# Hybrid DeltaNet step on one core: preparation steps of consecutive chunks on seven common places per chunk, scan steps behind four of them

## The chip, the core and the metric

The kernel runs as one program on one core of a Trainium2 chip. The metric is the device time in microseconds (us) of one execution; a lower time is better. The engines are named as the profile names them: PE (matmuls; PEld is its weight load), DVE and ACT (elementwise work), POOL, and SP, which issues every DMA of this kernel.

## The reference: what is computed

One layer of a diffusion backbone over 128 context tokens and 2048 latent tokens, 17 tiles of 128 tokens. Half of the mixer is a gated DeltaNet with 4 heads, run over the tokens in both directions; the other half is a gated spatial MLP. A projection, a second norm and a wide squared-ReLU MLP follow. The part that matters here is the DeltaNet:

```python
    a_mat = jnp.where(strict, jnp.einsum('bnhcd,bnhsd->bnhcs', k_beta, k) * decay, 0.0)
    rhs = jnp.concatenate([v * beta, k_beta * jnp.exp(g)[..., None]], axis=-1)
    sol = lax.linalg.triangular_solve(a_mat + jnp.eye(DN_CHUNK, dtype=f32), rhs,
                                      left_side=True, lower=True, unit_diagonal=True)
    u, w = sol[..., :DV], sol[..., DV:]
    qk = jnp.einsum('bnhcd,bnhsd->bnhcs', q, k) * decay
    ...
    def step(S, xs):
        qd, kd, u_c, w_c, qk_c, gl = xs
        v_new = u_c - jnp.einsum('bhck,bhkv->bhcv', w_c, S)
        o = jnp.einsum('bhck,bhkv->bhcv', qd, S) + jnp.einsum('bhcs,bhsv->bhcv', qk_c, v_new)
        S = S * jnp.exp(gl)[..., None, None] + jnp.einsum('bhck,bhcv->bhkv', kd, v_new)
        return S, o
```

For each chunk a triangular matrix is inverted, which does not need the state of the chunk before; then the state is carried on, which does.

## The kernel before

The program has three stages: modulation, norms and the q, k, v projections (to about 440 us); the DeltaNet stage (to about 1265 us); the MLP (to the end). The change lies in the second.

The kernel takes chunks of 128 tokens. A **unit** is one chunk in one direction; `units` holds 34: 17 forward (0 to 16), then 17 backward (17 to 33, the first of them the context tile). Each unit has 17 **preparation steps** (list `prep`, which invert the matrix) and 4 **scan steps** (list `scan`, which carry the state).

- Preparation: two steps that build the matrix (lines 985 to 1010); a transpose (line 1016); five doubling levels for widths 2, 4, 8, 16, 32, each of two steps; and four closing steps (lines 1066 to 1098). The first step of a level, called **Pa1 to Pa5** here, is four matmuls at line 1036, and DVE makes the tile `P` from them at line 1040. The second, **XY1 to XY5**, is eight matmuls at lines 1048 and 1050 that read `P`; ACT then casts `Y` and `X` (lines 1051, 1052), which the next Pa reads. At the end stand **R** (lines 1084, 1085) and **T** (lines 1094, 1095).
- Scan: **s0** (kT by the state; DVE updates `vt` at line 1108), **s1** (T by vt; ACT copies `vn`), **s2** (kt by vn; DVE makes the new state at line 1128), **s3** (16 matmuls at lines 1139 and 1140 that read `qT` and `QK`; this is the output).

Each unit loads its operands by DMA. `kt`, `kT`, `vt` and `qT` have two buffers each, so the `qT` of unit u+2 can be fetched only when s3 of unit u has read its own, and the `kt` of unit u+2 only after s2 of unit u. As soon as `qT` is there DVE multiplies it with the decay (line 1130), and ACT scales `kt` (line 1103).

All other work of the stage is **fill**: the gate and gMLP projections of all tiles, the output projection and the second norm, whose PE part is mostly matmuls of 512 columns at lines 220 to 222 (one group of three for each slice of 128 inputs).

What sets the order: every step is put on a list with a time in units of a chunk (`at(time, fn, kind)`); unit i has its chunk at time i. Before the change the 17 preparation steps of unit i are spread evenly over a window around i (`WINDOWS`: 2.43 chunks long up to unit 17, 2.69 from unit 18 on), and the 4 scan steps over a window of their own (1.57 and 1.18 chunks). The list is sorted by time and issued; a first matmul of fill is ordered behind the preparation or scan step issued last (from time 18 on: behind the fourth last). The recording layer then orders each engine's queue by its own estimate of when things are ready. Each engine works its queue strictly in that order, so an instruction that waits holds all behind it.

```python
            for j, st in enumerate(u["prep"]):
                at(i - w[0] + (j + 0.5) * (w[0] - w[1]) / n, st, "prep")
            spread(i + w[2], i + w[3], [scan_step(i, f) for f in u["scan"]], "chain")
```

Of the kernel before, what the change touches and what calls it, by code (L numbers as in the profile page):

```python
# [21 lines left out]
NT = 17  # L22
# [8 lines left out]
def interleave(*lists):  # L31
# [5 lines left out]
    for _, _, _, s in sorted(order, key=lambda e: e[:3]):  # L37
# [18 lines left out]
AHEAD = 3  # L56
WINDOWS = [2.46, 0.03, -0.51, 1.06, -1.61, 18.16, 17.58, 18.3,
           2.63, -0.06, -0.18, 1.0, 1.36, 1.64, 1.66, 2.66, 3.17, 3.71]


@with_exitstack
def hybrid_step(
# [144 lines left out]
    def w512(name, dt=F32):  # L207
        return wp.tile([P, 512], dt, tag="w", name=name)
# [61 lines left out]
    with ExitStack() as ph:  # L270
# [479 lines left out]
        for bi in range(len(BLOCKS)):  # L750
# [6 lines left out]
            at = {e: n for n, e in enumerate(order)}  # L757
            tile_of = {}
            for n, (gi, h) in enumerate(order):
                u = us[n] if bi == 0 and n < 3 else feature_tile(blk, bi, gi, h)  # L760
# [158 lines left out]
    with ExitStack() as ph:  # L919
# [337 lines left out]
        def o_loads(u):  # L1257
            t = u["t"]
            u["of"], u["ga"] = w512("of"), w512("ga")
            load(out=u["of"], in_=of_d[t * P : (t + 1) * P, :])  # L1260
            load(out=u["ga"], in_=gate_d[t * P : (t + 1) * P, :])
# [74 lines left out]
        def at(time, fn, kind=None):  # L1336
            events.append((time, len(events), fn, kind))

        def spread(t0, t1, steps, kind):
            for j, st in enumerate(steps):  # L1340
                at(t0 + (t1 - t0) * (j + 0.5) / len(steps), st, kind)

        def scan_step(i, f):
            def g():
                u = units[i]
                if "s" not in u:
                    u["s"] = None if i in (0, NT) else units[i - 1]["sn"] if i not in (1, NT + 1) else u["s0"]
                f()
            return g

        def after(i):

            d = 0 if i == 0 else 1
            store(out=new_state[0, 0, d].rearrange("h k v -> k h v"), in_=units[i]["sn"])
            s0 = q32("S", 2)
            load(out=s0, in_=state_delta[0, 0, d].rearrange("h k v -> k h v"))
            units[i + 1]["s0"] = s0

        p2, p3 = WINDOWS[:8], WINDOWS[8:]
        for i, u in enumerate(units):  # L1360
            w = p2 if i <= NT else p3
            at(i - 3 if i > PL else -10, u["prep_loads"])
            at(i - 1, u["scan_loads"])
            n = len(u["prep"])
            for j, st in enumerate(u["prep"]):
                at(i - w[0] + (j + 0.5) * (w[0] - w[1]) / n, st, "prep")
            spread(i + w[2], i + w[3], [scan_step(i, f) for f in u["scan"]], "chain")
            if i in (0, NT):
                at(i + w[2] + (w[3] - w[2]) * 0.7, lambda i=i: after(i))
            if i >= NT:  # L1370
                at(i, lambda u=u: o_loads(u))
                first, second = o_steps(u)
                spread(i + p3[4], i + p3[5], first, "fill")
                spread(i + p3[6], i + p3[7], second, "fill")
                if u["t"] > 8:
                    st = h2_steps(u["t"], pj, fraw, w512, fpart, fhalf, lambda u=u: u["x2"])
                    spread(i + p3[8], i + p3[9] + 0.2, st[:5], "fill")
                    spread(i + p3[9] + 0.2, i + p3[9] + 2.1, st[5:], None)
# [427 lines left out]
    for j, t in enumerate(range(8, -1, -1)):  # L1806
        st = h2_steps(t, bank, lambda: w512("junk"), w512)
# [5 lines left out]
    for p, (o, n, b) in enumerate(seq):  # L1813
        u = units[n]
# [118 lines left out]
```

## Time and profile before

| | |
|---|---|
| median of 3 runs | 2678.39 us (2676.0 to 2682.14) |
| profiled execution | 2678.03 us |
| its span, first to last instruction | 2676.3 us |
| PE busy in the span | 2622.4 us, 98% |
| DVE busy | 1792.8 us, 67% |
| ACT busy | 1245.4 us, 47% |
| granted PE clock, mean | 0.995 |

Idle time of PE is time in which no matmul runs; the views of waits name what it waited for. An idle stretch of DVE or ACT costs nothing by itself, unless a matmul stands behind what they are late with.

### The profile page before, as it was taken

The page shows a single profiled execution, that of the slowest core. Times are in us where ns is not written, and L with a number is a line of the kernel's source. Part 1 is how long each engine was busy: PE and PEld are TensorE (multiplying, and loading weights), DVE is VectorE, ACT ScalarE, POOL GpSimd, SP SyncE. Part 2 cuts the span into 40 slices and gives each one's busy share as a digit, 9 for nine tenths or more (in the row PEclk, how much of TensorE's full clock was granted, in tenths as well). Part 3 has the DMA queues.
Part 4 walks back from the last instruction along what each step waited for, and adds up shares of the span by engine and source line. Part 5 has one row for each costly group of instructions (what it writes and reads, how often), then busy time and mean ns, then how long its engine had stood idle before and what let it go on. Part 6 is the DMA issues. An engine that isn't in the chain of part 4 may idle for free.

```text
span 2676.3 us, 45017 instructions
## 1 busy us (share of the span) xinstructions
PE 2622.4 (98%) x15698; PEld 2187.8 (82%) x15698; DVE 1792.8 (67%) x3694; ACT 1245.4 (47%) x3092; POOL 224.8 (8%) x448
## 2 busy tenths in 40 slices
PE   8999999999999999999999999999999999999998
PEld 5999998788887777788888888888888787888887
DVE  5867656766666778875688885566565556774874
ACT  4655555555554657763355543333242432332441
POOL 3111112111111111110000000000000000000000
PEclk9999999999999999999999999999999999999999
DMA  8867539655454657985868887443369978776772
GB/s 298 278 207 222 187 109 284 193 165 158 155 163 147 209 181 253 288 283 181 291 201 240 247 300 223 114 122 104 106 190 372 326 268 307 268 251 210 235 259 88
DMA packets 569385, 580.89 MB, mean 217 GB/s; under 512 B 35692, under 2 KB 401692, under 8 KB 565574
## 3 DMA queue, kind: packets, MB, share of 16 engines
q1 hardware_dynamic: 569158, 578.03, 67.6%
q8 instruction: 123, 2.02, 0.3%
q14 instruction: 104, 0.85, 0.1%
HBM read 398.14 MB, written 179.74 MB: 216 GB/s over the span
## 4 chain that ended last, share of the span: by engine, by line
PE 86%; DMA 6%; DVE 5%; ACT 1%; issue 1%; SPq 1%; POOL 0%; DVEq 0%; POOLq 0%; ACTq 0%
PE f L222 17%; PE f L220 17%; PE f L221 17%; PE pj L220 6%; PE pj L222 6%; PE pj L221 6%; PE pd L966 3%; PE pm L220 1%; PE pm L221 1%; PE pm L222 1%; PE pt L578 1%; PE pd L1140 1%; PE pd L1139 1%; DMA hop_d<-opL 1%; DMA qT<-qT_d 1%
## 5 line engine op out<-in xcount | busy, mean ns | idle before, releaser
L220 PE MATMUL f<-hop,zH 128*128 128x512 f32 x960 | 376.5, 393 | 1.2 <-ACT zH L1449 1.2
L221 PE MATMUL f<-hop,zH 128*128 128x512 f32 x960 | 377.1, 393 | 0.0
L222 PE MATMUL f<-hop,zL 128*128 128x512 f32 x960 | 376.9, 393 | 0.0
L220 PE MATMUL f<-hop,wH 128*128 128x512 f32 x896 | 354.0, 396 | 0.0
L221 PE MATMUL f<-hop,wH 128*128 128x512 f32 x896 | 350.7, 391 | 0.0
L222 PE MATMUL f<-hop,wL 128*128 128x512 f32 x896 | 350.6, 392 | 0.0
L1449 ACT CAST zH<-zraw 128x512 fp32r<-128x512 f32 x240 | 146.9, 621 | 297.1 <-DVE zraw L1443 86.4
L220 PEld LDWEIGHTS f<-hop,zH 128*128 128x128 f32 x960 | 180.4, 188 | 43.7 <-ACT zH L1449 1.6
L222 PEld LDWEIGHTS f<-hop,zL 128*128 128x128 f32 x960 | 180.3, 188 | 42.0 <-issue 0.9
L221 PEld LDWEIGHTS f<-hop,zH 128*128 128x128 f32 x960 | 180.1, 188 | 41.8 <-issue 0.9
L1443 DVE TENSOR_TENSOR zL<-zraw,zH 128x512 fp32r<-128x512 f32 x240 | 162.7, 687 | 66.4 <-ACT zH L1449 52.6
L222 PEld LDWEIGHTS f<-hop,wL 128*128 128x128 f32 x896 | 168.2, 188 | 37.6
L221 PEld LDWEIGHTS f<-hop,wH 128*128 128x128 f32 x896 | 168.5, 188 | 35.2
L220 PEld LDWEIGHTS f<-hop,wH 128*128 128x128 f32 x896 | 168.5, 188 | 34.8
L220 PE MATMUL pj<-kH,wH 128*128 128x386 f32 (+2 forms) x568 | 190.0, 337 | 0.3 <-DVE kH L476 0.3
L222 PE MATMUL pj<-kH,wL 128*128 128x386 f32 (+2 forms) x568 | 190.2, 335 | 0.0
L221 PE MATMUL pj<-kL,wH 128*128 128x386 f32 (+2 forms) x568 | 189.4, 334 | 0.0
L177 POOL TENSOR_TENSOR r<-rsq,nhalf 128x1 f32<-128x1 f32 (+1 forms) x38 | 23.4, 617 | 1480.2 <-DVE rsq L176 1480.2
L1443 DVE TENSOR_TENSOR wL<-raw,wH 128x512 fp32r<-128x512 f32 x112 | 76.1, 687 | 74.7 <-ACT wH L1449 73.7
L526 DVE SCALAR_TENSOR_TENSOR cv<-pj,vec,cv 128x384 f32<-128x384 f32 (+2 forms) x164 | 87.1, 538 | 55.1 <-ACT cv L523 53.8
L220 PEld LDWEIGHTS pj<-kH,wH 128*128 128x128 f32 x568 | 107.2, 189 | 4.8 <-issue 4.2
L1449 ACT CAST wH<-s 128x512 fp32r<-128x512 f32 x96 | 59.3, 620 | 108.6 <-DVE s L1443 108.3
(398 smaller groups left out, 6036.1 us busy)
## 6 DMA issues: line engine op xcount, KB each, us to landing
zraw<-z_d SPq DMA_DIRECT2D x212, 256.0 KB
raw<-in_w_ff_dram SPq DMA_DIRECT2D x128, 256.0 KB
hop<-hop_d SPq DMA_DIRECT2D x28, 1024.0 KB
z_d<-c SPq DMA_DIRECT2D x96, 256.0 KB
zraw<-s_d SPq DMA_DIRECT2D x96, 256.0 KB
raw<-in_w_mod_dram SPq DMA_DIRECT2D x80, 256.0 KB
r<-in_w_ff_dram SPq DMA_DIRECT2D x80, 256.0 KB
s_d<-s SPq DMA_DIRECT2D x64, 256.0 KB
```

The costliest lines, as they stand in the source:

```text
L177: G.tensor_tensor(out=out, in0=t[:np_, :n], in1=nhalf[:np_, :n], op=ALU.pow)
L220: T.matmul(ps, lh, rh, start=first and i == 0, stop=False, skip_group_check=more)
L221: T.matmul(ps, lh, rl, start=False, stop=False, skip_group_check=more)
L222: T.matmul(ps, ll, rh, start=False, stop=last and i == n - 1, skip_group_check=more)
L526: V.scalar_tensor_tensor(out=cv[:, o : o + m], in0=ps[:, s + sh : s + sh + m], scalar=convw[:, w, j : j + 1], in1=cv[:, o : o + m], op0=AL ...
L578: T.matmul(ps[:, i * P : (i + 1) * P], kTt[:, i * P : (i + 1) * P], rhs[:, i * P : (i + 1) * P], start=True, stop=True)
L966: T.matmul(p[:, h, :], lhs[:, h, :], rhs[:, h, :], start=True, stop=True)
L1139: T.matmul(p[:, h, :], u["qT"][:, h, :], s[:, h, :], start=True, stop=False)
L1140: T.matmul(p[:, h, :], u["QK"][:, h, :], u["vn"][:, h, :], start=s is None, stop=True)
L1443: V.tensor_tensor(out=out, in0=a, in1=b, op=op)
L1449: A.copy(h, src)
```

## The change

The preparation steps now have a fixed pitch of one seventh of a chunk, for both directions. Step j of unit i+1 then has the very same time as step j+7 of unit i, so that the steps of up to three units are issued together, the older unit's first. The four scan steps no longer have a window; they are issued 0.1 place behind the preparation step at places 15, 18, 20, 23 (forward) or 16, 18, 20, 23 (backward), counted from the unit's own first place.

```diff
+PLACES = 7
+SCAN = ((15, 18, 20, 23), (16, 18, 20, 23))
...
             for j, st in enumerate(u["prep"]):
-                at(i - w[0] + (j + 0.5) * (w[0] - w[1]) / n, st, "prep")
-            spread(i + w[2], i + w[3], [scan_step(i, f) for f in u["scan"]], "chain")
+                at((i * PLACES + j + 0.5) / PLACES - w[0], st, "prep")
+            for j, f in zip(SCAN[i > NT], u["scan"]):
+                at((i * PLACES + j + 0.6) / PLACES - w[0], scan_step(i, f), "chain")
```

Up to unit 17 the pitch was 2.43/17 = 0.14294 chunk and is now 0.14286. From unit 18 on it was 2.69/17 = 0.158. In chunks from its unit's time i, the scan steps stood at -0.31, 0.08, 0.47, 0.86 forward and stand at -0.23, 0.20, 0.48, 0.91; backward they stood at -0.03, 0.26, 0.56, 0.85 and stand at -0.26, 0.03, 0.31, 0.74. The last preparation step of a backward unit stood at -0.02 and stands at -0.27. No instruction is added or removed; no size, buffer or engine changes. The line numbers of the changed kernel are 2 higher in the functions of the stage.

How the queues move, at the places of which the prediction speaks:

PE, forward, between the first level of unit 10 (AH_8920, X_8922) and the second step of that level, XY1, its first matmul the last row here. Before:

```order
L966 MATMUL pd_9043<-vt_8686,T_8988 128x128 x4
L220 MATMUL pj_8996<-wH_5468,hH_8731 128x512
L221 MATMUL pj_8996<-wL_5469,hH_8731 128x512
L222 MATMUL pj_8996<-wH_5468,hL_8735 128x512
L220 MATMUL pj_8996<-wH_5480,hH_8731 128x512
L221 MATMUL pj_8996<-wL_5481,hH_8731 128x512
L222 MATMUL pj_8996<-wH_5480,hL_8735 128x512
L1048 LDWEIGHTS X_8922
L1048 MATMUL pd_9056<-P2_5738,X_8922 128x64
```

Of the changed kernel, the same stretch, from the last matmul of Pa1 of unit 10 (AH_8929 there) to the first of Pa5 of unit 9 (AH_8606); the three further pairs of Pa5 follow, and then XY1 of unit 10:

```order
L1038 MATMUL pd_9035<-Y_8978,AH_8929 128x64
L222 MATMUL pj_8996<-wH_5468,hH_8724 128x512
L223 MATMUL pj_8996<-wL_5469,hH_8724 128x512
L224 MATMUL pj_8996<-wH_5468,hL_8728 128x512
L222 MATMUL pj_8996<-wH_5480,hH_8724 128x512
L223 MATMUL pj_8996<-wL_5481,hH_8724 128x512
L224 MATMUL pj_8996<-wH_5480,hL_8728 128x512
L1038 LDWEIGHTS AH_8606
L1038 MATMUL pd_9049<-Y_8651,AH_8606 128x64
```

Scan step s1 (line 966, tiles vt and T) stood ahead of XY1 with fill around it; it now stands behind XY1. Between Pa1 and XY1 stood XY4 of unit 9, s1 and six fills; now six fills and Pa5 stand there. Ahead of Pa1, back to s3 of unit 7, stood twelve fills, three of which were followed by a transpose step, Pa4 and T; now six fills and XY4 stand there.

DVE, forward, from the product of `qT` of unit 9 on (the tile P_5738 is that of level 1, P_5742 that of level 5). Before:

```order
L1130 TENSOR_TENSOR qT<-qT,gb 128x512
L1054 TENSOR_TENSOR QK<-QK,E 128x512
L1170 TENSOR_SCALAR gw<-gw 128x512
L1040 TENSOR_TENSOR P_5738<-pd,sm_183 128x128x2
L1171 TENSOR_TENSOR gw<-pj,gw 128x512
```

and of the changed kernel:

```order
L1132 TENSOR_TENSOR qT<-qT,gb 128x512
L1042 TENSOR_TENSOR P_5738<-pd,sm_183 128x128x2
L1056 TENSOR_TENSOR QK<-QK,E 128x512
L1042 TENSOR_TENSOR P_5742<-pd,sm_187 128x8x32
L1006 SCALAR_TENSOR_TENSOR KK<-KK,beta,Es 128x128 x4
```

The `P` that XY1 reads moved up to stand directly behind the product with `qT`.

DVE, backward, from the product of `qT` of unit 23 on. Before:

```order
L1130 TENSOR_TENSOR qT<-qT,gb 128x512
L1279 TENSOR_TENSOR r_13711<-r_13711,oss 128x4
L1054 TENSOR_TENSOR QK<-QK,E 128x512
L1319 TENSOR_TENSOR tmp<-pj,row 128x512
L868 TENSOR_TENSOR d<-y 128x512
L176 TENSOR_SCALAR rsq<-r_13711 128x4
L1320 TENSOR_TENSOR x<-x,tmp 128x512
L1004 SCALAR_TENSOR_TENSOR KK<-KK,beta,Es 128x128 x4
L1278 TENSOR_TENSOR r_15210<-rq 128x4
L1040 TENSOR_TENSOR P_5742<-pd,sm_187 128x8x32
```

and of the changed kernel:

```order
L1132 TENSOR_TENSOR qT<-qT,gb 128x512
L1280 TENSOR_TENSOR r_15228<-rq 128x4
L1321 TENSOR_TENSOR tmp<-pj,row 128x512
L1056 TENSOR_TENSOR QK<-QK,E 128x512
L1042 TENSOR_TENSOR P_5742<-pd,sm_187 128x8x32
```

The `P` of level 5 moved from the tenth row to the fifth.

ACT, backward, around the scaling of `kt` of unit 24. Before:

```order
L1078 CAST X<-pd 64x4x64
L862 CAST opH<-ev 128x512
L849 ACTIVATE ev<-pj,b_200,a_199 128x128 x4
L1103 ACTIVATE kt<-kt,eglg 128x128 x4
L1051 CAST Y<-pd 128x32x8
```

and of the changed kernel:

```order
L1080 CAST X<-pd 64x4x64
L1105 ACTIVATE kt<-kt,eglg 128x128 x4
L1301 CAST oH<-pj 128x512 x2
L1011 CAST AH<-KK 128x512
L851 ACTIVATE ev<-pm,b_200,a_199 128x128 x4
L1053 CAST Y<-pd 128x32x8
```

The scaling of `kt` moved ahead of the second norm's evictions (`ev`), and seven other instructions now stand between it and the cast of `Y` that the next matmul step of the preparation reads.

## The prediction

> **What bounds the kernel now.** I read the page's busy times first, then the windows by stage, then the waits of PE within the DeltaNet stage, then the waits of the two engines that feed it.
>
> ```profile
> PE 2622.4 (98%) x15698; PEld 2187.8 (82%) x15698; DVE 1792.8 (67%) x3694; ACT 1245.4 (47%) x3092; POOL 224.8 (8%) x448
> ...
> 440.00:540.00 100.00, 89.13 (x632) 69.42 (x631) 64.02 (x182) 52.54 (x137) 20.41 (x23) 0.93 0.72 224
> 540.00:895.00 355.00, 347.71 (x2930) 286.37 (x2929) 225.04 (x632) 190.88 (x507) 43.07 (x56) 0.99 0.53 162
> 895.00:1265.00 370.00, 353.17 (x3050) 288.71 (x3050) 281.82 (x711) 236.77 (x728) 53.66 (x65) 1.00 0.73 233
> 1265.00:2676.00 1411.00, 1401.44 (x6515) 1155.98 (x6513) 928.38 (x1513) 521.81 (x999) 17.80 (x27) 1.00 0.70 225
> ```
>
> The columns are the stretch, its length, busy time of PE, PEld, DVE, ACT and POOL, the clock, DMA share, GB/s. PE is the bound nearly everywhere, and the change removes no PE work. It can only move PE's idle time in the DeltaNet stage: 10.9 us in its start (540 less 440, less 89.13), 7.3 us forward, 16.8 us backward, 35 us in all, with a little clock on top. So the most to be won is about 1.5%; what can be lost has no such limit. The waits between 540 and 1265 us say what that idle time is:
>
> ```profile
> PE pd L1048 <- DVE P L1040: 15.1, 22, 2.0
> PE pd L1036 <- ACT Y L1051: 3.3, 8, 0.8
> ...
> DVE qT L1130 <- DMA qT<-qT_d: 36.0, 19, 4.3
> ...
> ACT kt L1103 <- DMA kt<-kt_d: 37.9, 25, 4.0
> ```
>
> PE waits for `P`, made by DVE, 15.1 of 24.1 us. DVE itself stands 36.0 us before the product with `qT`, for a DMA; ACT stands 37.9 us for `kt`. These stand early in their queues, long before s2 or s3 need them, and hold whatever is behind. One chunk shows the chain:
>
> ```profile
> 1005.14 0.53 SPq L979 DMA_DIRECT2D qT<-qT_d  x1
> ...
> 1011.27 0.69 DVE L1130 TENSOR_TENSOR qT<-qT,gb 128x512 f32<-128x512 f32 x1 [1.96 <-DMA qT<-qT_d]
> ...
> 1016.12 0.74 DVE L1040 TENSOR_TENSOR P<-pd,sm 128x256 f16<-128x256 f32 x2
> ...
> 1012.84 0.41 PE L1036 MATMUL pd<-Y,AH 128*128 128x64 f16 x8
> ...
> 1016.58 0.29 PE L1048 MATMUL pd<-P,X 128*128 128x64 f16 x4 [0.98 <-DVE P L1040]
> ```
>
> The fetch of `qT` starts when s3 of two units earlier lets go of the buffer and takes 6.1 us; DVE loses 1.96 us; `P`, whose matmuls were issued at 1012.84, comes only at 1016.12, and PE loses 0.98 us. The edit decides how much PE work covers such a chain.
>
> **The change part by part.** No instruction, DMA or wait is added. Three covers change.
>
> *The product with qT, forward.* I take room as PE's work from the end of s3 of unit u-2 to the XY in question, less DVE's work from the start of the `qT` product of unit u to the end of that XY's `P`. A fetch that lands later than its room makes PE wait for the difference. Unit 9, whose queues are shown above, before:
>
> ```profile
> 681.87 0.53 SPq L979 DMA_DIRECT2D qT<-qT_d  x1
> ...
> 685.29 0.69 DVE L1130 TENSOR_TENSOR qT<-qT,gb 128x512 f32<-128x512 f32 x1 [1.39 <-DMA qT<-qT_d]
> 685.95 0.69 DVE L1054 TENSOR_TENSOR QK<-QK,E 128x512 f32<-128x512 f32 x1
> ...
> 686.89 0.42 DVE L1040 TENSOR_TENSOR P<-pd,sm 128x256 f16<-128x256 f32 x1
> ...
> 681.82 0.47 PE L220 MATMUL pj<-wH,hH 128*128 128x512 f32 x1
> ...
> 682.60 0.40 PE L1016 MATMUL pd<-ident,X 128*128 128x128 f16 x4
> ...
> 685.47 0.29 PE L1036 MATMUL pd<-Y,AH 128*128 128x64 f16 x4
> 685.61 0.28 PE L1048 MATMUL pd<-P,X 128*128 128x64 f16 x4
> ...
> 685.84 1.14 PE L966 MATMUL pd<-vt,T 128*128 128x128 f32 x8
> 686.73 0.48 PE L220 MATMUL pj<-wH,hH 128*128 128x512 f32 x1
> ...
> 688.21 0.29 PE L1048 MATMUL pd<-P,X 128*128 128x64 f16 x4
> ```
>
> s3 ends at 681.82, XY1 comes at 688.21: 6.4 us of cover. `P` is ready at 686.89 + 0.42 = 687.31, so nothing waits. Now the stretch holds six fills (686.73 to 688.21: 1.48), XY4 (0.23), Pa1 (0.14), six fills (1.48), Pa5 (0.14): 3.47 us. XY1 is due 681.82 + 3.47 = 685.29, just when `qT` lands; `P` stands directly behind the product and is ready at 685.29 + 0.66 + 0.42 = 686.37. PE waits 1.1 us where it waited for nothing.
>
> The same count over units 3 to 16, with durations of such rows and the two orders, gives rooms before of 3.4, 3.5, 3.6, 4.4, 4.5, 4.6, 4.6, 4.8, 4.9, 4.9, 5.1, 5.7, 7.8, 7.8 us and now 1.9, 2.5, 2.9, 3.0, 3.3, 3.4, 3.5, 3.5, 3.5, 3.7, 4.0, 4.0, 5.3, 5.6. Landings of these units, as issue to start of a product that waited, or bounds, are about 3.3 us in nine, 4.2 in two, 5.2 in three:
>
> ```profile
> 614.63 0.53 SPq L979 DMA_DIRECT2D qT<-qT_d  x1
> ...
> 618.88 0.69 DVE L1130 TENSOR_TENSOR qT<-qT,gb 128x512 f32<-128x512 f32 x1 [2.20 <-DMA qT<-qT_d]
> ...
> 844.50 0.58 SPq L979 DMA_DIRECT2D qT<-qT_d  x1
> ...
> 849.76 0.69 DVE L1130 TENSOR_TENSOR qT<-qT,gb 128x512 f32<-128x512 f32 x1 [3.57 <-DMA qT<-qT_d]
> ```
>
> With this mix over each room the waits add up to 2.2 us before and 8.4 now: **+6 us**. All at 3.3 us gives +3; all at 5.2 gives +14.
>
> *The product with qT, backward.* `P` of level 5 stands nearer the product (2.5 us of DVE work instead of 5.3 for unit 23), but its XY5 comes much earlier: PE work from s3 falls from 10.7 to 7.1 us, since s3 and s0 are now adjacent and only one run of fills is left ahead of Pa5. Taking the tighter of XY5 and XY2, rooms were 3.7 to 5.4 us for units 20 to 29 and are 2.8 to 4.8. Unit by unit with its own landing (6.9, 3.4, 3.3, 6.1, 4.7, 4.8, 6.4, 4.3, 6.2, 3.5 for 20 to 29; those of 22, 24, 26, 28 are upper bounds) the waits are 2.6 to 7.0 us before, 10.5 to 14.3 now: **+8 us**, from +3 to +12 by those bounds.
>
> *The scaling of kt, backward.* It moved ahead of evictions on ACT, so the cast of `Y` that Pa4 needs has 4.6 us of ACT work behind the wait instead of 1.6 (unit 24). Rooms from s2 to Pa4 were 4.6 us or more and are 0.8 and 1.3 for units 20 and 19, then 2.8 to 4.3.
>
> ```profile
> 1093.19 0.89 SPq L981 DMA_DIRECT2D kt<-kt_d  x1
> ...
> 1096.87 0.99 ACT L1103 ACTIVATE kt<-kt,eglg 128x128 f32<-128x128 f32 x3 [1.19 <-DMA kt<-kt_d]
> ```
>
> This landing took 3.7 us; over the units they are 2.6 to 3.8. The waits come to **+5 us** (0 where the evictions end late anyway, 9 if each is 1 us later).
>
> The Trainium skill (DMA: Bandwidth & Descriptors, "Anatomy of one DMA") gives about 2.0 us of fixed cost plus bytes over 436 GB/s, so an estimate of 2.6 us for these 256 KB; the rows disagree with 3.4 to 6.1 us for `qT`. By its figure nearly all three terms would vanish.
>
> *Clock.* One wait of 2.01 us was followed by a stretch at two thirds of the clock:
>
> ```profile
> 829.65 0.28 PE L1048 MATMUL pd<-P,X 128*128 128x64 f16 x4 [2.01 <-DVE P L1040]
> ...
> 825.00:830.00 5.00, 2.99 (x35) 1.00 0.86 222
> 830.00:835.00 5.00, 5.00 (x31) 0.66 0.60 190
> ```
>
> That is 5 x 0.34 = 1.7 us more. Some six of the waits above reach 1.8 us, against two now; with half of them charged, **+3 us** (0 to 8). The Trainium skill (TensorE: Matmul & The Clock Gate, "The two states you'll see") lets the clock fall only after about 3.4 us of idleness, which would make this term nothing; the row shows it after 2.01.
>
> *What is won.* At the start s0 of unit 1 waits for the initial state:
>
> ```profile
> 516.65 1.76 PE L966 MATMUL pd<-S,kT 128*128 128x128 f32 x7 [1.49 <-DMA S<-in_state_delta_dram]
> ...
> 515.00:520.00 5.00, 3.51 (x17) 0.67 0.71 212
> ```
>
> R, XY3 and three more fills now stand ahead of it, about 1.2 us, and the slow clock (5 x 0.33) goes with the wait: **-3 us**. Runs of fill become fewer, 326 to 293 in the two orders; three fills take 0.78 us (681.82 to 682.60) and six 1.48, so a run costs 2 x 0.78 - 1.48 = 0.08: **-3 us**. Backward, two Pa stood together and then two XY (the x8 row at 1012.84), so ACT had four casts at once; now a Pa stands with an XY. That may free the 3.3 us that PE waits for `Y`: **-3 us**.
>
> Sum: 6 + 8 + 5 + 3 - 3 - 3 - 3 = +13 us. The profiled execution took 2678.0 us, 0.4 below the median of the three runs, so about **2691 us**. The low ends of the terms with all gains give -3 us, the high ends with no gain +43.
>
> **The rivals.** *Faster: the even mix of steps wins.* With one Pa and one XY at each place, DVE and ACT get half the burst, and PE's late `P` would go. For it: forward, where the steps already stood so, PE lost 7.3 us in 355, backward 16.8 in 370. It decides if fetches land within 3.3 us, as they do where DMA is less busy (3.4 us at 681.87). Then the waits shrink to about 8 us where 7 stand by the same count today, and the 9 us of gains remain, some of the other backward waits with them: 2678 - 9 - 2 = 2667 us. Against it: `qT` took 6.1 us at 1005.14. The skill's figure for a DMA points here.
>
> *Slower by more: the clock.* If nearly every chunk has a wait near 2 us, each costs 1.7 us more; 20 chunks make 34 us in place of 3: 2722 us. It decides from waits of about 2 us on; most of mine are 0.5 to 1.5.
>
> *No difference.* Forward the pitch hardly changes (0.14294 to 0.14286 chunk), so the steps already fell together, and the queues follow the recording layer's order and not the list. If the tighter covers and the gains are equal, it stays at 2678.
>
> **How the numbers follow.** The likeliest case has 0.55 (its own range 2684 to 2704), the faster one 0.20, no difference 0.13, the clock 0.12. About 0.2% either way, 5 us, is what a measurement tells from no change here; slower then has 0.67, same 0.13, faster 0.20. The range reaches into the faster case and up to most of the clock's: 2664 to 2718 us.
>
> **What would show it.** Right: more waits for `P` of line 1050 (1048 before, 15.1 us), a longer stand of DVE for `qT` (36.0), forward idle time well over 7.3 us, XY1 late by 1 us near unit 9, Pa4 waiting backward, and the 1.49 us wait for S nearly gone. Wrong: PE's idle time between 540 and 1265 us at or below 24 us, or landings of `qT` below 3.3 us throughout.

## The result and the profile after

The changed kernel takes 2720.17 us (median of five runs, 2714.56 to 2721.77), the kernel before 2682.14 us in the same series (2676.0 to 2683.6). The ratio is 1.0136 with a 95% interval of 1.0121 to 1.0151: slower by 1.36%. The profiled execution's span grew from 2676.3 to 2717.7 us, by 41.4 us. The forecast of 2691 us, 13 us more, had the direction and the place right and the size wrong; 2720 us lies above its range, which ended at 2718 us.

The windows by stage of the changed kernel, columns as before; its stage ends at about 1310 us:

```profile
440.00:540.00 100.00, 88.57 (x625) 68.21 (x623) 62.59 (x181) 52.42 (x136) 21.71 (x23) 0.91 0.71 220
540.00:895.00 355.00, 340.64 (x2865) 277.53 (x2861) 219.03 (x625) 189.66 (x498) 40.87 (x56) 0.99 0.52 157
895.00:1310.00 415.00, 376.00 (x3143) 311.36 (x3142) 289.61 (x724) 246.91 (x747) 58.83 (x66) 0.96 0.69 216
```

PE's idle time from 540 us on was 24.1 us and is 14.4 + 39.0 = 53.4 us. The clock of the last window, 1.00 before, is 0.96. The waits in the same stretch (what waited, for whom; us in total, times, longest):

```profile
DVE qT L1132 <- DMA qT<-qT_d: 48.7, 24, 7.0
ACT kt L1105 <- DMA kt<-kt_d: 44.5, 26, 4.3
...
PE pd L1050 <- DVE P L1042: 37.2, 31, 3.7
...
DVE o L1148 <- PE pd L1142: 24.1, 12, 4.4
...
DVE QK L1056 <- DMA QK<-qk_d: 6.6, 6, 2.5
...
PE pd L1068 <- ACT Y L1053: 3.7, 6, 2.1
```

PE waits for `P` 37.2 us instead of 15.1. DVE stands 48.7 us for `qT` (36.0), ACT 44.5 us for `kt` (37.9).

Where the 41.4 us lie. Forward and backward are parted at s0 of unit 18; an idle stretch is put to the step whose matmul ends it; the clock's loss is the sum over slices of 5 us of 5 us times what the granted clock lacked to 1, for the start and from 540 us to the stage's end.

| | before | after | difference |
|---|---|---|---|
| PE idle, start (440 to 540 us) | 10.9 | 11.4 | +0.5 |
| PE idle, forward | 10.4 | 19.0 | +8.5 |
| PE idle, backward | 13.7 | 34.4 | +20.7 |
| of it at XY2 and XY5 | 6.1 | 21.1 | +15.0 |
| lost to the clock, start | 6.8 | 8.5 | +1.7 |
| lost to the clock, from 540 us on | 3.4 | 18.8 | +15.4 |
| what is left of 41.4 us | | | -5.4 |

Forward, the worked example of the prediction can be looked up. The timeline of the changed kernel at XY1 of unit 10 (start, length, instruction; in brackets the idle time ahead of it and what ended that):

```profile
689.31 0.53 SPq L981 DMA_DIRECT2D qT<-qT_d  x1
...
694.35 0.69 DVE L1132 TENSOR_TENSOR qT<-qT,gb 128x512 f32<-128x512 f32 x1 [2.97 <-DMA qT<-qT_d]
694.96 0.42 DVE L1042 TENSOR_TENSOR P<-pd,sm 128x256 f16<-128x256 f32 x1
...
695.43 0.28 PE L1050 MATMUL pd<-P,X 128*128 128x64 f16 x4 [2.58 <-DVE P L1042]
```

The chain is the one that was told, link by link, but PE waits 2.58 us where 1.1 us had been worked out. The cover came out as told: 3.59 us of PE work from the end of s3 to XY1, where 3.47 us had been added up. The fetch took 5.04 us, and not the 3.4 us that were carried over from the kernel before. Backward, one piece of 13 us shows one stand at work on two steps:

```profile
1074.26 0.69 DVE L1148 TENSOR_TENSOR o<-pd,of 128x512 f32<-128x512 f32 x1 [1.22 <-PE pd L1142]
1074.33 0.58 SPq L981 DMA_DIRECT2D qT<-qT_d  x1
...
1080.25 0.69 DVE L1132 TENSOR_TENSOR qT<-qT,gb 128x512 f32<-128x512 f32 x1 [2.45 <-DMA qT<-qT_d]
...
1082.06 0.42 DVE L1042 TENSOR_TENSOR P<-pd,sm 128x256 f16<-128x256 f32 x1
...
1082.53 0.28 PE L1050 MATMUL pd<-P,X 128*128 128x64 f16 x4 [1.51 <-DVE P L1042]
...
1085.93 0.68 DVE L870 TENSOR_TENSOR d<-y 128x512 f32<-128x512 f32 x1
...
1086.53 0.41 DVE L1042 TENSOR_TENSOR P<-pd,sm 128x256 f16<-128x256 f32 x1
1087.00 0.28 PE L1050 MATMUL pd<-P,X 128*128 128x64 f16 x4 [2.12 <-DVE P L1042]
```

`qT` lands 5.9 us after its issue. DVE stands 2.45 us, and from then on works without a gap until 1086.94. One stand makes two `P` late, that of XY5 by 1.51 us and that of XY2, 4 us of DVE work further on, by 2.12 us. The prediction's count gives the sum: from the fetch to the XY2, PE works 1087.00 - 1074.33 - 1.51 - 2.12 = 9.0 us and DVE, from the product on, 6.7 us, so the room is 2.4 us, and a landing of 5.9 us leaves 3.6.

### The profile page after: what moved, and what is told of

It reads as the page before. It is cut to its first block, busy times and chain, and to the rows that moved or that the text cites. A ratio compares the mean times of both kernels' runs of the same rounds, so it can differ in the third digit from the quotient of the medians.

```text
span 2717.7 us, 45048 instructions
## 1 busy us (share of the span) xinstructions
PE 2633.7 (97%) x15698; PEld 2197.2 (81%) x15698; DVE 1791.8 (66%) x3694; ACT 1251.9 (46%) x3092; POOL 227.1 (8%) x448
## 4 chain that ended last, share of the span: by engine, by line
PE 83%; DMA 7%; DVE 5%; ACT 2%; issue 2%; SPq 1%; POOL 0%; DVEq 0%; POOLq 0%; ACTq 0%
PE f L224 17%; PE f L222 17%; PE f L223 17%; PE pj L222 6%; PE pj L224 6%; PE pj L223 6%; PE pd L968 3%; DMA qT<-qT_d 2%; PE pm L222 1%; PE pm L223 1%; PE pm L224 1%; PE pd L1141 1%; PE pd L1142 1%; PE pt L580 1%; DMA QK<-qk_d 1%
## 5 line engine op out<-in xcount | busy, mean ns | idle before, releaser
L1053 ACT CAST Y<-pd 128x256 f16<-128x256 f32 x170 | 63.4, 373 | 99.4 <-PE pd L1052 98.4
```

Source lines behind the costliest of these rows:

```text
L1053: A.copy(y, py)
```

## The experiments

Each kernel was timed against the kernel before on the same chip; ratios are to it, with 95% intervals. Each expectation numbers its own theories.

**Which stand.** First the products that DVE and ACT stand for were ordered later, without moving a step. `behind` runs a function and orders what it issues behind a given instruction of the same engine; `newest` is the engine's instruction that was written last.

a_q_late: in the changed kernel, the product with `qT` behind the update of the state in the same scan step.

```diff
-                    V.tensor_tensor(out=u["qT"], in0=u["qT"], in1=u["eg"], op=ALU.mult)
+                    behind(lambda: V.tensor_tensor(out=u["qT"], in0=u["qT"], in1=u["eg"], op=ALU.mult),
+                           newest(mybir.EngineType.DVE))
```

> The changed kernel, with the product of qT put behind the update of the state on DVE (same unit, same step), so that DVE meets it long after its fetch has landed. Theory 1 (PE lost its time because DVE stood for the qT fetch with P behind it, with less cover than before): DVE's wait for qT falls from 48.7 us to under 5, PE's wait for P from 37.2 to under 15, the clock loss goes with it, and the time falls from 2720 to about 2685 us. Theory 2 (DVE has too much work per chunk behind too little PE cover, whatever it waits for): PE's wait for P stays over 28 us and the time over 2708.

Measured: 2709.55 us, 1.0099 (1.0084 to 1.0114). Its waits:

```profile
DVE QK L1068 <- DMA QK<-qk_d: 42.9, 22, 3.9
...
ACT kt L1117 <- DMA kt<-kt_d: 27.8, 23, 3.7
...
ACT E L1005 <- DMA gb<-g_d: 23.0, 21, 3.3
...
PE pd L1062 <- DVE P L1054: 17.0, 12, 2.7
...
PE pd L1050 <- ACT Y L1065: 15.6, 12, 2.3
```

The stand for `qT` is gone. DVE now stands 42.9 us for `QK` (6.6 in the changed kernel) and ACT 23.0 us for g's factor. The two factors share a set of buffers, so a late `qT` product also lets the next g be fetched later: between 560 and 760 us g's fetch starts 0.03 us after that product in both kernels, 14 to 17 us ahead of its first reader (E, on ACT) in the changed kernel and 3 to 4 us in this one. The stand had moved to the next fetch. The time fits theory 2 (over 2708 us); PE's wait for `P`, 17.0 us and not over 28, does not.

a_k_late: in the changed kernel, `kt`'s scaling in scan step s1, behind T's evictions on ACT.

> The changed kernel, with the scaling of kt put behind the evictions of T of the same unit on ACT (emitted in s1 instead of s0). If the stand of ACT for the kt fetch costs PE what the prediction charged (5 us, up to 9), the time falls from 2720 to about 2713 and the waits of Pa4 and XY3 backward (4.7 us by the trace) go. If it costs nothing, since evictions end late anyway, it stays within 3 us of 2720.

Measured: 2688.96 us, 1.0027 (1.0016 to 1.0039). By the ratios 1.09% of the 1.36% went, some 29 us, several times what the prediction had put on `kt`. PE's idle time from 540 us on is 36.2 us (53.4 in the changed kernel), the clock's loss 6.8 us (18.8).

a_qk_late: both edits.

> The changed kernel with both moves. Theory 1: about 2680 us, near or below the kernel before, since then neither engine stands for a fetch with preparation work behind it. Theory 2: over 2700.

Measured: 2708.49 us, 1.0094 (1.0077 to 1.011). This is above the 2700 us of theory 2. DVE stands 51.1 us for `QK`, ACT 43.9 us for g.

b_q_late: the edit of a_q_late in the kernel before.

> The kernel before with the same move of the qT product. Theory 1: PE's wait for P falls from 15.1 us to about 6 and the time by 8 to 12 us, to about 2671. Theory 2: no more than 3 us.

Measured: 2686.97 us, 1.0016 (1.0007 to 1.0025), with a stand of 29.3 us for `QK` and 27.9 us for g: nothing is gained in the kernel before either.

**Which half, which part of the edit.** e_fwd2 and e_bwd2 take the new places in one direction only (for e_fwd2 `i <= NT`, for e_bwd2 `i > NT`), e_prep2 takes the pitch of the preparation steps alone, e_scan2 the places of the scan steps alone.

```diff
-                at((i * PLACES + j + 0.5) / PLACES - w[0], st, "prep")
+                at((i * PLACES + j + 0.5) / PLACES - w[0] if i <= NT else
+                   i - w[0] + (j + 0.5) * (w[0] - w[1]) / n, st, "prep")
```

> The new places for units 0 to 17 alone; units 18 to 33 stand where they stood before. Theory 1 (the backward half pays, where ACT stands for kt ahead of the casts): up to s0 of unit 18 as in the changed kernel, 6.2 us later than before (927.6 against 921.4), and from there as before, 342 us; about 2689 us, ratio 1.0024. Theory 2 (waits near 2 us and the clock that they cost, alike in both halves): about half of the 38 us, 2701 us, ratio 1.007.

Measured: 2688.07 us, 1.003 (1.0019 to 1.004).

> The new places for units 18 to 33 alone. Theory 1: from s0 of unit 18 to the end some 370 to 378 us (342.0 before, 377.7 in the changed kernel), up to it as before; 2710 to 2718 us, ratio 1.0105 to 1.013. Theory 2: half of the 38 us, 2701 us, ratio 1.007. If the halves don't add up to the 38 us, something is handed over between them.

Measured: 2707.48 us, 1.0103 (1.008 to 1.0127). The halves add up, 0.30% and 1.03% against 1.36%, and the backward one pays three quarters. It comes a little below the range given.

> The new places of the preparation steps alone; scan steps stand in their old windows. In ACT's queue kt's scaling of units 24, 28 and 30 then has the four cast instructions of line 849 and the cast of line 862 ahead of it, and not behind it as in the changed kernel. Theory 1 (kt on ACT is the price): most of the loss goes, 2684 to 2694 us, ratio 1.001 to 1.0045. Theory 2 (the common pitch of the preparation steps makes P, Y and X late): 2705 us or more, ratio above 1.0085.

Measured: 2712.48 us, 1.0122 (1.0106 to 1.0137), nearly the whole loss. The theory that `kt` on ACT is the price falls here. But the other one is not shown by it either, as the timeline of e_prep2 tells:

```profile
1095.31 0.69 DVE L1056 TENSOR_TENSOR QK<-QK,E 128x512 f32<-128x512 f32 x1 [3.58 <-DMA QK<-qk_d]
...
1096.25 1.06 DVE L865 TENSOR_TENSOR opL<-ev,opH 128x512 fp32r<-128x512 f32 x1
...
1100.96 0.68 DVE L1321 TENSOR_TENSOR tmp<-pm,row 128x512 f32<-128x512 f32 x1
...
1101.56 0.41 DVE L1042 TENSOR_TENSOR P<-pd,sm 128x256 f16<-128x256 f32 x1
...
1102.03 0.37 PE L1050 MATMUL pd<-P,X 128*128 128x64 f16 x4 [3.78 <-DVE P L1042]
```

DVE stands 3.58 us, this time for `QK`, and then has 5.6 us of work ahead of the `P` of XY5. Backward, 28.4 us of PE's idle time is at XY5 in this kernel. Of the stretches there of 0.8 us or more, 16.4 us have a stand for `QK` as DVE's longest stand for a fetch just ahead of them, 10.4 us one for `qT`.

> The new places of the scan steps alone; preparation steps stand as before. kt's scaling of units 20 to 30 stands right behind a level's two casts, ahead of the casts of lines 849, 1068 and 1078. Theory 1: most of the loss stays, 2705 to 2720 us, ratio 1.0085 to 1.014. Theory 2 (the pitch of the preparation steps): 2680 to 2690 us, ratio below 1.003.

Measured: 2703.43 us, 1.0092 (1.0074 to 1.0109), between the two ranges. Each part alone costs most of the loss, and each at other steps. So a third theory was formed: what costs is any product on a fetched operand that stands in DVE's or ACT's queue while its fetch is under way, whichever it is; the places only decide which `P` or cast stands behind it.

**Without the fetches.** a_nofetch is the changed kernel without the fetches of `kt`, `qT` (and its factor) and `QK`; b_nofetch the same of the kernel before; a_nokt leaves out `kt`'s alone. `n` numbers the units.

```diff
+                if n < 3:
+                    kept["QK", n] = q32("QK", 3)
+                    load(out=kept["QK", n], in_=qk_d[t])
+                u["QK"] = kept["QK", n % 3]
...
+                    if nm in ('kt', 'qT') and n > 1:
+                        u[nm] = kept[nm, n % 2]
+                        continue
+                    u[nm] = kept[nm, n] = q32(nm, 2)
```

> The changed kernel, in which kt, qT and QK are fetched for the first two or three units alone (and qT's factor too); later units keep what the buffer holds, and the product for qT is a maximum with itself. All casts, products and matmuls remain and keep their order to a few places; only the three fetches that DVE and ACT stand for are gone. Theory A (what costs is DVE and ACT standing in order for fetched tiles, ahead of a P or a cast): the idle of PE from 540 us on falls from 53 us to 25 us or less, the time is within 0.4 % of b_nofetch. Theory B (the places themselves: P, Y and X come too late because steps of several units fall together): it stays 20 us or more above b_nofetch.

> The kernel before with the same three fetches left out, as the measure for a_nofetch. Theory A: some 10 to 20 us below the kernel before, since its own stands for qT and QK (36 us and 9 us on DVE) go too, of which some 11 us show on PE. Theory B: within 5 us of the kernel before.

Measured: a_nofetch 2679.78 us, 0.9998 (0.9988 to 1.0008); b_nofetch 2656.79 us, 0.9919 (0.9905 to 0.9934). Without its fetches PE hardly idles in the kernel before, as its windows show:

```profile
540.00:895.00 355.00, 354.55 (x3022) 292.16 (x3018) 238.67 (x667) 202.14 (x536) 46.70 (x60) 1.00 0.40 124
895.00:1310.00 415.00, 405.35 (x3242) 333.68 (x3241) 304.59 (x749) 250.62 (x750) 55.13 (x63) 1.00 0.64 208
```

Forward idle time of a_nofetch is 4.3 us (19.0 in the changed kernel) and of b_nofetch 0.4 us (10.4 in the kernel before), so forward the orders are 3.9 us apart instead of 8.5: there the fetches explain more than half of the loss. But 23 us stay between the two kernels, more than theory A allows and as much as theory B had named (20 us or more). The timeline of a_nofetch at XY2 of unit 28 says what they are:

```profile
1098.05 0.32 SPq L832 DMA_DIRECT2D y<-h_d  x1
...
1101.42 0.69 DVE L870 TENSOR_TENSOR d<-y 128x512 f32<-128x512 f32 x1 [5.16 <-DMA y<-h_d]
1102.03 0.42 DVE L1050 TENSOR_TENSOR P<-pd,sm 128x256 f16<-128x256 f32 x1
1102.50 0.37 PE L1058 MATMUL pd<-P,X 128*128 128x64 f16 x4 [4.46 <-DVE P L1050]
```

A fourth fetch, `y` of the second norm. Its product `d` stands right ahead of the level-2 `P`; in the changed kernel DVE comes there too late to wait for it. Four such stands lie right ahead of 14.3 of the 16.0 us at XY2 backward, and each of the four waits is followed by 3.4 us at half clock, 1.7 us more.

> The changed kernel, in which kt alone is fetched for the first two units only; its scaling stays on ACT at its place ahead of the casts. Theory A (ACT's stand for the fetch is the price): about 2689 us like a_k_late, ratio 1.001 to 1.005. Theory C (the four scalings' own 1.2 us or so of work ahead of the casts is the price, and a_k_late gained by moving that work): 2708 us or more.

Measured: 2701.71 us, 1.008 (1.0065 to 1.0095), between both. `kt`'s fetch is worth 0.56%, 15 us. The 14 us more that a_k_late gained come from moving the scaling's work, or from the few places by which the queues shift when it moves; the two were not parted.

b_k_late: the edit of a_k_late in the kernel before.

> The kernel before with kt's scaling behind T's evictions on ACT. ACT stands 37.9 us for kt there, but only 1 us of PE's idle follows such a stand. Theory A: 2670 to 2682 us, ratio 0.996 to 1.000; below before at most by the 1 us and its clock, and what the fetches behind gain. Theory C: the same or slower, as the scaling then stands ahead of vn's eviction.

Measured: 2683.78 us, 1.0016 (1.0007 to 1.0026). Slower than theory A gives, as theory C allows. Idle time at XY5 backward stays (5.3 us, 5.2 before), but 4.5 us of it now follow a stand for `y`, and Pa5 waits 4.8 us backward (1.8 before).

a_nofetch_d: a_nofetch with `d` ordered behind the third product of its list.

> a_nofetch, with d (line 870, the difference of the two halves of y) ordered behind the third product of its own step list, so that DVE no longer stands for y's fetch ahead of P of the second level. Theory A (every stand for a fetch in DVE's and ACT's order counts, y's too): the 16.0 us of idle at XY2 backward go, 2656 to 2668 us, ratio 0.991 to 0.996. Theory B (the places): 2675 us or more.

Measured: 2662.38 us, 0.9926 (0.991 to 0.9943). The idle time at XY2 is gone, and the interval overlaps that of b_nofetch: without most of the stands for fetches the two orders differ by 0.07% where they differed by 1.36%. The two are not quite alike, as `d` was moved in one alone; DVE stands 2.9 us for `y` in b_nofetch. The moved product also shifts its neighbours, so the 0.72% between a_nofetch and this kernel is not the stand's alone.

**The whole kernels without running ahead.** The runs above also took traffic from the DMA engines. a_still (changed kernel) and b_still (kernel before) fetch everything, and only keep three products from running ahead: behind what is written ahead of them, that of `QK` one level on (not two, as the expectation has it), and that with `qT` written in s0 instead of s2.

```diff
+                behind(scaled, newest(mybir.EngineType.Activation))
...
+                    behind(lambda: V.tensor_tensor(out=u["qT"], in0=u["qT"], in1=u["eg"], op=ALU.mult),
+                           newest(mybir.EngineType.DVE))
...
-                    if s == 2:
-                        V.tensor_tensor(out=u["QK"], in0=u["QK"], in1=u["E"], op=ALU.mult)
+                    if s == 4:
+                        behind(lambda: V.tensor_tensor(out=u["QK"], in0=u["QK"], in1=u["E"], op=ALU.mult),
+                               newest(mybir.EngineType.DVE))
```

> The changed kernel whole, with the three products kept from running ahead: kt's scaling behind ACT's last instruction written ahead of it, qT's product behind vt's products in the same scan step, QK's product two levels on behind that level's P. Each still ends some 20 us ahead of its reader. Theory A: 2660 to 2692 us, the stands for qT, QK and kt together under 40 us (105 us in the changed kernel), unless the fetch behind qT's in the queue (g) takes their place as in a_q_late. Theory B: above 2700 us.

> The kernel before with the same three orders. Theory A: 2660 to 2682 us, below the kernel before by up to 20 us. If g's fetch takes the stand over as in b_q_late: 2682 to 2692 us.

Measured: a_still 2679.32 us, 0.9991 (0.9982 to 1.0); b_still 2672.86 us, 0.9964 (0.9951 to 0.9977), faster than the kernel before and the changed one. The waits of a_still:

```profile
ACT E L1005 <- DMA gb<-g_d: 36.7, 24, 3.3
...
PE pd L1081 <- ACT Y L1065: 21.4, 13, 2.4
...
DVE d L870 <- DMA y<-h_d: 12.0, 4, 3.8
...
DVE QK L1068 <- DMA QK<-qk_d: 3.1, 1, 3.1
...
PE pd L1062 <- DVE P L1054: 2.3, 2, 2.0
```

No stand for `qT` or `kt` is left, 3.1 us for `QK`, and PE waits 2.3 us for `P` instead of 37.2. The two orders are 6.5 us apart, where they were 38 us apart. What remains is ACT's stand for g's factor, ahead of the cast for which step Pm (line 1081, lines 1066 and 1068 of the kernels before and after) waits: backward 14.4 of its 19.3 us follow such a stand.

a_still2 and b_still2 put the first operation on that factor (E) behind ACT's last instruction written ahead of it, too.

> a_still, and the first operation on g's fetched factor (E, on ACT) is ordered behind ACT's last instruction written ahead of it too. Theory A: the 21.4 us for which PE waits at Pm (line 1081 of a_still) fall to under 8 us and the time to 2655 to 2670 us, ratio 0.991 to 0.996. Theory B (a remainder that lies in the places): 2675 us or more.

> b_still with the same order for E. Theory A: 2658 to 2670 us, ratio 0.992 to 0.996, since 12.5 us of PE's idle follow a stand for g in b_still; a_still2 within 5 us of it. Theory B: 2672 us as b_still.

Measured: a_still2 2757.7 us, 1.0284 (1.0261 to 1.0306); b_still2 2695.12 us, 1.005 (1.0035 to 1.0065). Both missed. The waits of a_still2:

```profile
POOL Es L1012 <- ACT E L1010: 342.4, 29, 25.4
...
PE pd L1034 <- DVE X L1028: 52.0, 26, 3.4
```

The stand for g is gone, but E has a near reader: POOL, then DVE's `KK`, ACT's `AH`, DVE's `X` and the transpose on PE (line 1034) wait for it in turn. The other three had room: in the changed kernel `kt`'s scaling starts 43.0 us ahead of s2, the product with `qT` 42.7 us and that of `QK` 65.4 us ahead of s3 (medians over the units), in a_still still 17.4, 21.6 and 57.2 us.

The loss of b_still2 is another matter. From 540 us on its idle time is 22.7 us, where b_still has 24.6. One wait of 19.8 us for `X` at the stage's start (to 483.37 us) makes up most of the 22 us between the two: there E of the first unit stands on ACT behind casts of weights, which wait for fetches of their own. a_still2 has this wait too, 20.4 us. So what E's new place costs later in the stage is shown for the changed order alone.

## Why the prediction was right or wrong

The terms added up to +13 us, and 41.4 us came; 28 us are missing. The step of the prediction that failed is the clock term, +3 us: 15.4 us were measured from 540 us on, and 1.7 us more in the start. Two gains of 3 us each were not won, and backward 20.7 us of idle time came where the terms hold 8 + 5 - 3 = 10.

- **What bounds it, and direction: right.** No work was added or removed, and of the 29.3 us by which PE's idle time grew from 540 us on, 22.1 us are its waits for `P`.
- **The product with qT, forward, +6 us: right in mechanism, a little small.** Idle time grew by 8.5 us, 5.3 of them at XY1, and the half alone costs 9 us.
- **The product with qT, backward, +8 us ("from +3 to +12"): right in mechanism, inside its range.** For the units 20 to 29, of which it speaks, the waits at XY2 and XY5 grew from 4.9 to 16.2 us, by 11.3. "Taking the tighter of XY5 and XY2" was the right count, as 1074 to 1087 us shows: the tighter room gives the sum of both waits. Three of the tightest rooms were smaller than its 2.8 us (2.4, 2.4 and 1.5 us).
- **Backward waits without a term.** Of the 21.1 us at XY2 and XY5, 14.4 follow a stand for `qT`, but 3.7 one for `QK`, which had no price.
- **The scaling of kt, +5 us ("0 to 9"): inside its range as idle time, on another path.** Without its fetch the time falls by 15 us; in the profiles 7.9 us of that is idle time of PE and 6.9 us clock. The term looked at Pa4, which waits 1.3 us backward, and none of that follows a stand for `kt`. Two waits that do, of 1.73 us at 947.81 and 1.95 us at 1095.69 us, are of the output projection: ACT casts its operand `oH` behind the scaling, and in the second case DVE stands 3.0 us for that cast, with the product `tmp` that PE waits for behind it.
- **The clock, +3 us ("0 to 8"): mis-sized, 15.4 us.** "Some six of the waits above reach 1.8 us" was near: eight do, three before. What failed is "half of them charged", at 1.7 us each. From 540 us on the changed kernel has eleven intervals of 3.41 us at half clock, against two. They also follow waits of 1.68 and 1.73 us and three short ones in a row (0.55, 0.47 and 0.64 us), and two waits were followed by two intervals each. The rival that put the loss on the clock named 2722 us, next to the measured time, but by luck: its picture, a wait near 2 us in nearly every chunk, was half right, as 15 of the 41 us are clock and 30 are idle time. The rule cited in that term, that the clock falls only after about 3.4 us of idleness (Trainium skill, TensorE: Matmul & The Clock Gate, "The two states you'll see"), is not borne out: one of the 13 waits of 1.5 us or more is that long. The last section shows what else counts.
- **The start, -3 us: not won, +2.2.** s0 of unit 1 waits 0.31 us for the state instead of 1.49, but the transpose step waits 2.57 us (0.99 before) and s3 of unit 0 now 1.29, and the clock loses 1.7 us more. Something else is late next, which the term did not ask.
- **The waits for Y, -3 us: not won.** From 540 us on Pa waits 2.4 us for the casts of `Y` instead of 3.3, but step Pm 3.7 us instead of 0.2.
- **Fewer runs of fill, -3 us: fits in sign** the -5.4 us that the table leaves over; it was not tried by itself.
- **The faster rival: refuted.** Its even mix of steps brought no more than the 0.9 us at Pa. Landings of `qT` stayed at 3.3 to 6.5 us, with which it had been argued away. The Trainium skill's figure for a DMA (DMA: Bandwidth & Descriptors, "Anatomy of one DMA"), an estimate of 2.6 us for these 256 KB, stays below them; its fit is one for DMAs issued through the gpsimd path, and these are issued by SP.
- **"No difference"** was right about one thing: with the stands for `qT`, `QK` and `kt` taken out, the two orders lie within 7 us of each other (a_still and b_still).

## What to carry to other kernels

An operation on a fetched operand belongs in an in-order queue where its fetch has long landed, not where its buffer has just come free, as long as its reader has the room (40 us and more here; E had none in the changed order). Before changing an order, list every operation in it that waits for a DMA and all that the bounding engine needs from the work behind it, since one stand makes everything behind it late. Take such stands out together: with `qT`'s taken out alone, DVE stood for `QK` and ACT for g instead. And price a wait of some 2 us of the bounding PE together with the clock that it may cost, here 1.7 us and twice that in two cases.

## What the hardware showed

A PE idle for about 2 us is not always followed by a lower clock. Three slices of the changed kernel, with the clock in the third column from the right:

```profile
695.00:700.00 5.00, 4.57 (x28) 4.20 (x28) 4.03 (x12) 1.24 (x3) 1.91 (x3) 0.67 0.47 114
...
1085.00:1090.00 5.00, 3.00 (x30) 2.58 (x30) 3.50 (x11) 1.31 (x4) 1.03 (x1) 1.00 0.57 173
1090.00:1095.00 5.00, 3.74 (x39) 3.23 (x37) 1.17 (x3) 2.53 (x7) 0.00 (x0) 1.00 0.08 30
```

The wait of 2.58 us at 695.43 is followed by 0.67. That of 2.12 us at 1087.00 is followed by a full clock, in its own slice and the next. In the kernel before, of two waits of 2.01 us one was followed by 0.66 and the other, at 906.90 us, by a full clock, so the length of a wait alone does not tell.

Most of what decides can be read from the traces, though no run was made for it. The stretches at half clock last 3.413 us or a whole multiple of it. The ten of the changed kernel between 445 and 1310 us begin at 464.56, 696.67, 843.44, 939.01, 949.25, 1031.17, 1096.03, 1140.40, 1167.71 and 1177.95 us, all on one grid of that pitch. The same waits by intervals of this grid:

```profile
693.26:696.67 3.41, 1.24 (x17) 1.00 0.16 59
696.67:700.08 3.41, 3.41 (x15) 0.50 0.61 141
...
1082.38:1085.79 3.41, 2.25 (x22) 1.00 0.92 245
1085.79:1089.20 3.41, 2.21 (x27) 1.00 0.44 124
```

The columns are PE's busy time, the clock, DMA share and GB/s. The first wait has 2.17 us of idleness in one interval, and the next interval runs at half clock. The second is split by a boundary into two intervals, which have 1.16 and 1.20 us, and nothing follows. In the interval ahead of each of the ten stretches PE idled 1.65 to 2.51 us; no other interval at full clock has more than 1.69 us. In the kernel before it is 1.49 to 2.01 us against at most 1.52. In other runs the border is less sharp (in b_q_late two stretches follow 0.75 and 1.07 us, and 1.86 us had none), so a fixed limit is not shown.

The same section of the Trainium skill has the activity counted in windows of 3413 ns that run freely, and the grid agrees with it.
